# Row-wise infinity norm: most loads moved from SyncE to GpSimd, one packet per DMA engine and load

## The chip, the cores and the metric

The kernel runs on one core of a Trainium2 chip. The metric is the device time of one execution in microseconds, lower being better. The kernel before took 627.58 us, the median of three runs (627.51 to 627.71).

The engines are called PE (TensorE), DVE (VectorE), ACT (ScalarE), POOL (GpSimd) and SP (SyncE). SP computes nothing here; it issues DMA transfers. Sixteen DMA engines move the data from HBM into SBUF, the on-chip memory of 128 partitions.

## The reference

```python
def setup_inputs():
    return {
        "x": np.random.randn(8192, 8192).astype(np.float32),
    }

def reference(x: np.ndarray) -> np.ndarray:
    return np.linalg.norm(x, ord=np.inf, axis=1)
```

With `axis=1` this is a vector norm: for each of the 8192 rows, the largest absolute value of its 8192 columns. The input is 8192 x 8192 x 4 bytes = 268.44 MB, the output 32 KB. Every byte is read once and takes part in one comparison.

## The kernel before

Each partition holds 64 rows of x: 46 from a first group and 18 from a second one (`GROUPS`). "Row 0 to 63" below means the row within a partition; one row for all 128 partitions is 4 MB. The rows pass through a ring of 3 x 16384 floats per partition. `WHOLE` and `LAST` give the widths of the loads in columns, and behind each width the parts that ScalarE and GpSimd take over from VectorE near the end.

```python
GROUPS = [46, 18]
WHOLE = (
    [(8192, ())] * 2 + [(16384, ())] * 29 + [(16384, (3712, 3680)), (8192, (2016, 1984))]
)
LAST = [
    (3920, (1680,)), (1984, (848,)), (1040, (432,)), (576, (240,)), (320, ()), (352, ())
]
RING = 3 * 16384
```

One load is one DMA of 128 partitions, and for each partition one run of `w` floats that lie together in HBM (64 KB for 16384 columns). The last 352 columns go into a tile of their own, beside the partial results.

```python
    def load(pos, w):
        row = pos // n_cols
        a = pos - first[row] * n_cols
        if pos + w == R * n_cols:
            buf = last[:, :w]
        else:
            at = loads[-1][0] + loads[-1][1] if loads else 0
            if at + w > RING:
                at = 0
            buf = ring[:, at : at + w]
        inst = nc.sync.dma_start(out=buf, in_=x_of[first[row]][:, a : a + w]).ins
        ...   # cut: dependencies between loads that the reduces order anyway
        return buf
```

VectorE reduces each piece with one instruction (`absmax`, a tensor_reduce with max over absolute values). It is line 68 in the profile, the load is line 108.

```python
    pos = 0
    for u, (w, g) in enumerate(WHOLE):
        buf = load(pos, w)
        ...   # cut: row and number of rows
        if whole:
            red = absmax(
                res[:, row : row + whole],
                buf[:, : whole * n_cols].rearrange("p (c m) -> p c m", m=n_cols),
            )
        if g:
            ...   # cut: the last two whole loads are shared with ScalarE and GpSimd

    n = LAST[-1][0]
    for h, (w, g) in enumerate(LAST[:-1]):
        buf = load(pos, w)
        pos += w
        shared(last[:, n : n + 1 + len(g)], buf, g)
        n += 1 + len(g)

    load(pos, LAST[-1][0])
    absmax(res[:, R - 1 :], last)
    final = nc.sync.dma_start(out=out_of[first[-1]][:, GROUPS[-1] - 1 :], in_=res[:, R - 1 :])

    for f, o in out_of.items():
        k = min(o.shape[1], R - 1 - f)
        early = keep(nc.scalar.dma_start(out=o[:, :k], in_=res[:, f : f + k]))
        ...   # cut: a scheduling order against `final`
```

A load of 16384 columns can only be issued when the reduce of the load three before it has freed its part of the ring. The helper `keep` holds an instruction in program order; the loads of SP are not held by it, so the scheduler may move one that waits for nothing.

Of the kernel before, what the change touches and what calls it, by code (L numbers as in the profile page):

```python
# [1 line left out]

# [4 lines left out]

P = 128
FP32 = mybir.dt.float32
INT32 = mybir.dt.int32  # L10
MAX = mybir.AluOpType.max
X = mybir.AxisListType.X
ABS = mybir.ActivationFunctionType.Abs
# [11 lines that stand above are left out]
    (3920, (1680,)), (1984, (848,)), (1040, (432,)), (576, (240,)), (320, ()), (352, ())  # L25
]
RING = 3 * 16384


@with_exitstack  # L30
def kernel(
    ctx: ExitStack,
    tc: tile.TileContext,
    x: bass.AP,
    out: bass.AP,
):
    nc = tc.nc
    n_rows, n_cols = x.shape
    R = n_rows // P
    assert R == sum(GROUPS) and n_cols == 8192  # L40
    keep = tc.keep_in_program_order


    first = []
    x_of, out_of = {}, {}
    for k in GROUPS:
        f = len(first)
        x_of[f] = x[f * P : (f + k) * P].rearrange("(p r) m -> p (r m)", r=k)
        out_of[f] = out[f * P : (f + k) * P].rearrange("(p r) -> p r", r=k)
        first += [f] * k  # L50

    single = ctx.enter_context(tc.tile_pool(name="single", bufs=1))

    ring = single.tile([P, RING], FP32)
    res = single.tile([P, R], FP32)

    n_parts = sum(1 + len(g) for w, g in LAST[:-1])
    last = single.tile([P, LAST[-1][0] + n_parts], FP32)

    def not_before(inst, other, why):  # L60
        tc.add_manual_dep(
            inst.ins, other.ins.name,
            mybir.DependencyInfo(mybir.DependencyClass.Sync, mybir.DependencyReason.DATA),
            reason=why,
        )

    def absmax(dst, src):
        return keep(nc.vector.tensor_reduce(  # L68
            out=dst, in_=src, axis=X, op=MAX, apply_absolute_value=True,
        ))  # L70

    def max_pool(dst, src):

        pool = nc.gpsimd
        keep(pool.add_instruction(  # L75
            mybir.InstTensorReduce(
                name=nc.get_next_instruction_name(),
                ins=[pool.lower_ap(src.bitcast(INT32))],
                outs=[pool.lower_ap(dst.bitcast(INT32))],
                op=MAX,  # L80
                axis=X,
            )
        ))

    def shared(part, buf, g):

        a = buf.shape[1] - sum(g)
        red = absmax(part[:, :1], buf[:, :a])
        for i, c in enumerate(g):
            keep(nc.scalar.activation(buf[:, a : a + c], buf[:, a : a + c], ABS))  # L90
            max_pool(part[:, 1 + i : 2 + i], buf[:, a : a + c])
            a += c
        return red

    loads = []
# [9 lines that stand above are left out]
            if at + w > RING:  # L105
                at = 0
            buf = ring[:, at : at + w]
        inst = nc.sync.dma_start(out=buf, in_=x_of[first[row]][:, a : a + w]).ins  # L108
        if pos + w < R * n_cols:
            if (len(loads) + 4) % 10 < 5:  # L110


                for b, v, earlier in loads:
                    if b < at + w and at < b + v:
                        tc.declare_no_dep(
                            inst, earlier, reason="ordered by the reduces in between",
                        )
            loads.append((at, w, inst))
# [6 lines that stand above are left out]
        row, k = pos // n_cols, w // n_cols  # L125
        pos += w
        whole = k - 1 if g else k
# [6 lines that stand above are left out]
            part = single.tile([P, 1 + len(g)], FP32, name=f"part{u}")  # L134
            shared(part, buf[:, whole * n_cols :], g)
            max_pool(res[:, row + whole : row + k], part)
        if u == 1:

            not_before(
                keep(nc.scalar.activation(res[:, :1], res[:, :1], ABS)),  # L140
                red, "not before the second row is in",
# [9 lines that stand above are left out]

    load(pos, LAST[-1][0])
    absmax(res[:, R - 1 :], last)
    final = nc.sync.dma_start(out=out_of[first[-1]][:, GROUPS[-1] - 1 :], in_=res[:, R - 1 :])


    for f, o in out_of.items():
        k = min(o.shape[1], R - 1 - f)
        early = keep(nc.scalar.dma_start(out=o[:, :k], in_=res[:, f : f + k]))
        tc.add_manual_dep(  # L160
            early.ins, final.ins.name,
            mybir.DependencyInfo(
                mybir.DependencyClass.NoSync, mybir.DependencyReason.SCHED_ONLY
            ),
            reason="takes the later semaphore",
        )


# [1 line left out]
_INS = ['x']  # L170
_OUTS = [((8192,), 'float32')]


# [23 lines left out]
```

## Time and profile before

| What | Value |
|---|---|
| Time, median of three runs | 627.58 us |
| Span of the profiled execution | 625.7 us |
| Bytes read from HBM | 268.44 MB |
| Mean rate over the span | 429 GB/s |
| VectorE busy | 536.7 us |
| First whole-row reduce starts | 12.85 us |
| Last reduce starts, lasts | 622.86 us, 0.53 us |

The profile page has the busy time of each engine, the span cut into 40 slices with a digit of busy tenths each, the DMA queues with their packets, and the chain of work that ended last, followed back from the final instruction. Below that stand groups of instructions: how often, the mean duration of one, and how long the engine sat idle before them and for whom. "Issue to landing" of a DMA runs from the instruction that starts it to the last of its completion signals. Times in the views count from the start of the span.

### The profile page before, as it was taken

How to read it: one execution, taken by the hardware profiler on the slowest of the kernel's cores; microseconds unless marked ns; L12 is line 12 of the kernel's file. 1: busy time of each engine (PE TensorE's matmuls, PEld its weight loads, DVE VectorE, ACT ScalarE, POOL GpSimd, SP SyncE). 2: the span in 40 equal slices, each digit the busy share in tenths (PEclk: the TensorE clock that was granted, in tenths of full speed). 3: DMA queues.
4: the chain of work that ended last, by engine and by line, in shares of the span. 5: the costliest groups of instructions: out<-in, count | busy, mean ns of one | idle time of the engine just before them, and what ended most of it. 6: DMA issues, size and time to landing. Idle time of an engine off the chain costs nothing.

```text
span 625.7 us, 175 instructions
## 1 busy us (share of the span) xinstructions
DVE 536.7 (86%) x40; ACT 15.1 (2%) x10; POOL 14.1 (2%) x14
## 2 busy tenths in 40 slices
DVE  1938988889888899888898888988889888899888
ACT  0000000000000000000000000000000000000044
POOL 0000000000000000000000000000000000000026
DMA  8999999999999999999999999999999999999997
GB/s 369 436 469 402 469 402 469 402 469 402 469 402 457 415 415 457 402 469 402 469 402 469 402 469 402 469 402 453 419 415 457 402 469 402 469 402 469 402 436 304
DMA packets 6048, 268.47 MB, mean 429 GB/s; under 512 B 1056, under 2 KB 1312, under 8 KB 1696
## 3 DMA queue, kind: packets, MB, share of 16 engines
q1 hardware_dynamic: 5760, 268.44, 99.3%
q10 hardware_dynamic: 288, 0.03, 0.0%
HBM read 268.44 MB, written 0.03 MB: 429 GB/s over the span
## 4 chain that ended last, share of the span: by engine, by line
DMA 71%; DVE 28%; SPq 0%; issue 0%; DVEq 0%
DMA ring<-in_x_dram 71%; DVE res L68 28%; DVE last L68 1%; SPq L108 0%; DVEq L68 0%
## 5 line engine op out<-in xcount | busy, mean ns | idle before, releaser
L68 DVE TENSOR_REDUCE res<-ring 128x2 f32<-128x16384 f32 (+1 forms) x32 | 525.4, 16420 | 86.4 <-DMA ring<-in_x_dram 86.4
L90 ACT ACTIVATE ring<-ring 128x3712 f32<-128x3712 f32 (+7 forms) x8 | 13.6, 1719 | 577.2 <-DMA ring<-in_x_dram 573.9
L75 POOL TENSOR_REDUCE part<-ring 128x1 int32<-128x3712 int32 (+3 forms) x4 | 10.1, 2562 | 607.6 <-ACT ring L90 607.6
L68 DVE TENSOR_REDUCE part<-ring 128x1 f32<-128x800 f32 (+1 forms) x2 | 5.5, 2748 | 0.1
L68 DVE TENSOR_REDUCE last<-ring 128x1 f32<-128x2240 f32 (+4 forms) x5 | 5.3, 1115 | 0.1
L75 POOL TENSOR_REDUCE last<-ring 128x1 int32<-128x1680 int32 (+3 forms) x4 | 3.4, 855 | 0.6 <-ACT ring L90 0.4
L140 ACT ACT_TABLE_LOAD x1 | 1.3, 1283 | 0.7 <-PEq L181 0.7
L140 ACT ACTIVATE res<-res 128x1 f32<-128x1 f32 x1 | 0.2, 203 | 29.3 <-DVE res L68 29.3
L68 DVE TENSOR_REDUCE res<-last 128x1 f32<-128x361 f32 x1 | 0.5, 529 | 0.1
L75 POOL TENSOR_REDUCE res<-part 128x1 int32<-128x3 int32 x2 | 0.4, 198 | 0.1
L181 POOL MEMSET const-float32-0.0<- 128x1 f32 x1 | 0.1, 99 | 0.2 <-issue 0.2
L181 POOL MEMSET const-bfloat16-1.0<- 128x1 bf16 x1 | 0.1, 102 | 0.0
L181 POOL MEMSET const-uint8-127<- 128x1 uint8 x1 | 0.1, 101 | 0.0
L181 POOL MEMSET const-float32-1.0<- 128x1 f32 x1 | 0.1, 99 | 0.0
## 6 DMA issues: line engine op xcount, KB each, us to landing
ring<-in_x_dram SPq DMA_DIRECT2D x3, 4096.0 KB, 21.4
ring<-in_x_dram SPq DMA_DIRECT2D x1, 1960.0 KB, 35.4
ring<-in_x_dram SPq DMA_DIRECT2D x1, 992.0 KB, 37.4
ring<-in_x_dram SPq DMA_DIRECT2D x1, 520.0 KB, 38.2
ring<-in_x_dram SPq DMA_DIRECT2D x30, 40.8
ring<-in_x_dram SPq DMA_DIRECT2D x1, 288.0 KB, 38.4
last<-in_x_dram SPq DMA_DIRECT2D x1, 176.0 KB, 38.3
ring<-in_x_dram SPq DMA_DIRECT2D x1, 160.0 KB, 38.3
```

The lines of the kernel that those rows point to most:

```text
L68: return keep(nc.vector.tensor_reduce(out=dst, in_=src, axis=X, op=MAX, apply_absolute_value=True,))
L75: keep(pool.add_instruction(mybir.InstTensorReduce(name=nc.get_next_instruction_name(), ins=[pool.lower_ap(src.bitcast(INT32))], outs=[poo ...
L90: keep(nc.scalar.activation(buf[:, a : a + c], buf[:, a : a + c], ABS))
L140: keep(nc.scalar.activation(res[:, :1], res[:, :1], ABS)),
L181: nc = _bacc.Bacc("TRN2", target_bir_lowering=False, num_devices=1)
```

## The change

Three things change.

The loads of rows 0 to 51 are issued by GpSimd in place of SP, with `single_packet=True`: the eight pieces (one for each partition) that a DMA engine moves for a load are marked as one packet in place of eight.

The very first load is cut: SP loads its first 512 columns (`BRIDGE`) while GpSimd prepares the other 7680. SP also keeps the loads of the last 12 rows.

The order in which the three output stores are written down is turned around, and the manual scheduling order between them is dropped.

It is for the gaps between packets: the DMA engines are to move longer stretches without a break, and SP's small load is to bridge the time until GpSimd's first data flows.

```diff
+SOFT = 52 * 8192
+BRIDGE = 512
...
-        inst = nc.sync.dma_start(out=buf, in_=x_of[first[row]][:, a : a + w]).ins
+        src = x_of[first[row]][:, a : a + w]
+        if pos == 0:
+
+            inst = nc.sync.dma_start(out=buf[:, :BRIDGE], in_=src[:, :BRIDGE]).ins
+            loads.append((at, BRIDGE, inst))
+            at, w, buf_, src = at + BRIDGE, w - BRIDGE, buf[:, BRIDGE:], src[:, BRIDGE:]
+        else:
+            buf_ = buf
+        if pos < SOFT:
+
+            inst = keep(nc.gpsimd.dma_start(out=buf_, in_=src, single_packet=True)).ins
+        else:
+            inst = nc.sync.dma_start(out=buf_, in_=src).ins
...
-    final = nc.sync.dma_start(out=out_of[first[-1]][:, GROUPS[-1] - 1 :], in_=res[:, R - 1 :])
-
...
-        early = keep(nc.scalar.dma_start(out=o[:, :k], in_=res[:, f : f + k]))
-        tc.add_manual_dep(
-            early.ins, final.ins.name,
-            mybir.DependencyInfo(
-                mybir.DependencyClass.NoSync, mybir.DependencyReason.SCHED_ONLY
-            ),
-            reason="takes the later semaphore",
-        )
+        keep(nc.scalar.dma_start(out=o[:, :k], in_=res[:, f : f + k]))
+    keep(nc.sync.dma_start(out=out_of[first[-1]][:, GROUPS[-1] - 1 :], in_=res[:, R - 1 :]))
```

In the built program of the changed kernel SP's instructions stand in this order: the 512 columns, the last 352 columns of the input (they go into a tile of their own and wait for nothing), five loads of 16384 columns, one of 8192, the tail of 3920, 1984, 1040, 576 and 320 columns, and the final store. Before, the 352 columns were the last load of all.

## The prediction

> **What bounds the kernel now.** I read the page from the top: busy time by engine, the 40 slices, the DMA queues, then the chain that ended last; after that the waits, the instruction groups by shape, and the packet records of the trace for the cost of one packet.
>
> ```profile
> DVE 536.7 (86%) x40; ACT 15.1 (2%) x10; POOL 14.1 (2%) x14
> ...
> DMA  8999999999999999999999999999999999999997
> ...
> DMA packets 6048, 268.47 MB, mean 429 GB/s; under 512 B 1056, under 2 KB 1312, under 8 KB 1696
> ...
> q1 hardware_dynamic: 5760, 268.44, 99.3%
> ```
>
> VectorE is the busiest compute engine, but the row of nines says that the 16 DMA engines never rest, from the first slice to the last but one. One queue carries everything: 268.44 MB, which is the whole of x. The queue's packet time covers 99.3% of the span, so what is left to gain by filling holes is under 1%.
>
> ```profile
> 59.16 0.02 issue
> 59.17 40.78 DMA ring<-in_x_dram
> 99.95 0.02 issue
> 99.97 17.23 DVE res L68
> 117.20 0.02 issue
> ...
> 582.02 35.44 DMA ring<-in_x_dram
> 617.45 0.02 issue
> 617.47 5.30 DVE last L68 x5
> 622.77 0.03 DVEq L68
> 622.81 0.05 issue
> 622.86 0.53 DVE res L68
> ```
>
> In the chain of work (start, duration, what) the same pattern comes back every 58.05 us: a load that takes 40.78 us from issue to landing, then a reduce of 17.23 us that frees its third of the ring. 58.05 us is three loads, so one load of 128 x 16384 floats (8.389 MB) takes 19.35 us. The load is issued with 40.78 - 19.35 = 21.4 us of other loads still ahead of it in the queue; an issue that is a few us late leaves no hole. The chain shows VectorE at 28% only because a reduce sits between two issues, not because it limits.
>
> ```profile
> DVE res L68 <- DMA ring<-in_x_dram: 86.4, 32, 12.8
> ...
> L68 DVE TENSOR_REDUCE res<-ring 128x2 f32<-128x16384 f32 x29 | 499.4, 17220 | 70.3 <-DMA ring<-in_x_dram 70.3
> L68 DVE TENSOR_REDUCE last<-ring 128x1 f32<-128x2240 f32 x1 | 2.5, 2485 | 0.1
> ```
>
> Here the waits and the groups by shape: a reduce of 17.22 us per 19.35 us load, so VectorE waits 2.13 us for each load. It sets the end only after the 3920-column load has landed (617.45): from there its five tail reduces run without a hole until the final one.
>
> Now the packets. In the trace's records a packet of 65,536 bytes takes 2418 ns, one of 2304 bytes 93 ns, one of 1280 bytes 55 ns, the 4-byte one that ends a load on each engine 9 ns. From 1280 to 65,536 bytes the slope is (2418 - 55)/64,256 = 0.03677 ns per byte, 27.2 GB/s per engine, 435 GB/s for 16. What is left is a constant of about 8.3 ns per packet (55 - 47.1). Eight packets and the ending one make 8 x 2418 + 9 = 19,353 ns, the 19.35 us of the chain. So the whole loss against the rate inside a packet is 9 x 8.3 = 75 ns a load, 0.4%.
>
> **What the Trainium skill says.** "DMA: Bandwidth & Descriptors", section "Where 436 GB/s comes from", puts the ceiling of a core's 16 DMA engines at 435 GB/s; the slope above agrees. Its section "Why small descriptors are slow (HBM only)" gives a fixed overhead of about 3 cycles per packet, which joining descriptors into one packet amortizes, beside a descriptor cost that joining does not remove. At that page's 850 MHz three cycles are 3.5 ns, less than half of the 8.3 ns that I find, so an estimate from this page is that not all of it goes away. Section "Queues, rings and completion order" says that an engine takes turns between queues at the ends of packets; no trace of the kernel before has two load queues, so it is untested here. "SBUF — State Buffer", section "Who interferes with whom", says that a tensor_reduce on this chip never takes the port that GpSimd needs to write descriptors; before, no load comes from GpSimd, so the trace says nothing of it.
>
> **The change part by part.**
> 1. Joined packets. Rows 0 to 51 are 27 loads on GpSimd (one of 7680, one of 8192, 25 of 16384 columns). Each has 8 packets per engine and would have one. If the whole 8.3 ns goes for 7 of 8: 27 x 7 x 8.3 = 1.57 us. If only the page's 3.5 ns goes: 27 x 7 x 3.5 = 0.66 us. If the cost belongs to the descriptor: 0. I take the middle of the first two, 1.1 us. It is wholly on the path, since the loads are.
> 2. Issue. 27 issues leave SP (0.33 us each) for GpSimd, whose generation is slower. With 21.4 us of loads ahead of each one, nothing of it shows, except at the start.
> 3. The start. Before, SP issues at 0.74 us and the first packet starts at 1.74 us. After, SP still does this, with 512 columns: 8 packets of 2048 bytes per engine, 8 x (75.3 + 8.3) + 9 = 0.68 us. The order of the instructions shows one thing that the diff does not say: the load of the last 352 columns has no wait and is now SP's second instruction, ahead of all others. It adds 8 x 60 + 9 = 0.49 us on the engines (60 ns is its packet in the records). Together they cover 1.17 us, to about 2.9 us. GpSimd issues at about 0.74 us as well; if its first data comes within 2.2 us of that, there is no hole. I expect none, or 0.2 us.
> 4. The 352 columns moved to the front. The end was set by VectorE from the landing of the 3920 columns on. Their landing now has 352 columns more ahead of it: 352 x 512 bytes at 434 GB/s = 0.42 us. The tail reduces after it are unchanged (5.30 + 0.09 + 0.53 us), and the data behind it ends earlier, which VectorE can't use. So this costs 0.42 us, unless the start had a hole that it fills. The cut of the first load adds 8 packets and an end, 0.08 us.
> 5. The junction. SP issues row 52 while GpSimd's last load is still queued. If engines take turns by packet, one 64 KB packet of SP (2.42 us) goes ahead of that load, which lands 2.42 us later; the next, short of that packet, lands 16.9 us after it. VectorE (17.22 us a reduce) is late by some 2.4 us once and regains it at 2.13 us a load with five loads left; the engines do not stop. Cost 0.
> 6. The last outputs: SP's final 0.5 KB store is unchanged in place; 0.
>
> Sum: -1.1 + 0.42 + 0.08 + 0.1 for the start = -0.5 us, 627.1. Not credited in it are the ending packets: if they join the load's packet as well, 27 x 8.3 ns = 0.22 us more goes. And a hole at the start of 0.4 us without the 352 columns would make them free. I lean a little to that side: 626.7 us.
>
> **The rivals.**
> A. The cost is per descriptor, or reading descriptors from memory costs as much as the joining saves. Then the load stays at 19.35 us, and the sum is +0.4 to +0.6: 628.1 us. For it: the skill's split of the two costs. Against: the 4-byte packet alone costs 9 ns, which looks like a price per packet.
> B. The first GpSimd packet (7680 columns in one piece, 8 x 30,720 bytes, 9 us on an engine) begins before SP's eight small packets are done on some engine. With turns by packet, each remaining small one then waits for a whole load; the 512 columns would land after several loads, VectorE would start tens of us late, the ring would fill, and the engines would stop for one or two reduces (8.7 to 17.4 us): 636 to 645 us. For it: packet starts of the first load are spread by 0.58 us over the engines in the kernel before. Against: SP's instruction is short and GpSimd has to write its descriptors first, and the width of 512 looks chosen for this.
> C. GpSimd starts late, beyond 2.9 us: each us is a hole of a us on the DMA path. A start at 4 us would make 628 us.
> D. The junction stops the ring: a large packet holds back SP's loads long enough for VectorE to starve twice. The slack of 21.4 us speaks against it; 1 to 3 us at most.
>
> **Range and chances.** The best case is parts 1 whole plus the ending packets, 1.8 us, and no other cost: 625.8; with a better start 625.4. A and a late start give 628 to 629. The range of 625.4 to 629.6 us leaves out B, which I give 5%. Over 2% faster would be below 615.0 us, while 268.44 MB at 435 GB/s alone are 617 us: 1%. Over 2% slower is 640.1 us and needs the bad form of B: 4%.
>
> **What would show it.** Step 1: the distance between VectorE's reduces in the GpSimd stretch (19.35 us now; 19.29 if the whole cost goes, 19.35 under A). Step 2: no holes in the DMA row. Step 3: the first 128 x 8192 reduce starts at 12.85 us now; 12.9 to 13.6 with both small loads ahead, 20 or more under B; the rise up to there gives a late start. Step 4: no hole in VectorE after the 3920 columns. Step 5: one wait of about 4.5 us near row 52, then shorter ones. I am wrong if the distance rises above 19.35 us or if VectorE is left waiting at the start.

## The result, and the profile after

The changed kernel takes 637.9 us (637.68 to 638.23, four runs) against 627.64 us for the kernel before, measured beside it (627.51 to 627.92, four runs). The ratio is 1.0163, with a 95% interval of 1.0146 to 1.0181. It is 10.3 us slower; the prediction said 626.7, with a range up to 629.6.

First the page of the kernel after: VectorE's and the DMA engines' busy tenths in 40 slices, the bytes moved per slice, and the two load queues (packets, MB, share of 16 engines' time).

```profile
DVE  0938988889888889888899888898888807999998
...
DMA  9999999999999999999999999999999999899992
GB/s 357 437 453 412 445 449 412 457 408 449 420 441 453 404 457 408 449 429 433 453 404 457 408 449 441 420 457 400 457 412 445 445 416 457 346 461 416 441 404 114
...
q0 software_dynamic: 3888, 217.84, 79.2%
q1 hardware_dynamic: 2016, 50.60, 18.6%
```

Two things differ from the rows of before. VectorE has a 0 near the end, and after it nines nearly up to the end: an engine that first had nothing to do and then could not catch up. The DMA engines' rate falls to 346 GB/s in one slice and to 114 in the last: the loads are done before VectorE is. GpSimd's queue counts 3888 packets, 27 loads x 16 engines x 9. Eight data packets and an end per engine and load are still in the records, as before. That they are joined into one packet is what the change asks for; no line of this page shows it.

The timeline of VectorE in the kernel after (start, duration, and in brackets the idle time before and who ended it):

```profile
15.52 8.69 DVE L72 TENSOR_REDUCE res<-ring 128x1 f32<-128x8192 f32 x1 [15.52 <-DMA ring<-in_x_dram]
25.22 8.69 DVE L72 TENSOR_REDUCE res<-ring 128x1 f32<-128x8192 f32 x1 [1.02 <-DMA ring<-in_x_dram]
44.58 17.22 DVE L72 TENSOR_REDUCE res<-ring 128x2 f32<-128x16384 f32 x1 [10.67 <-DMA ring<-in_x_dram]
...
470.36 17.22 DVE L72 TENSOR_REDUCE res<-ring 128x2 f32<-128x16384 f32 x1 [2.14 <-DMA ring<-in_x_dram]
489.72 17.22 DVE L72 TENSOR_REDUCE res<-ring 128x2 f32<-128x16384 f32 x1 [2.14 <-DMA ring<-in_x_dram]
528.44 94.32 DVE L72 TENSOR_REDUCE res<-ring 128x2 f32<-128x16384 f32 x6 [21.50 <-DMA ring<-in_x_dram]
622.67 5.40 DVE L72 TENSOR_REDUCE part<-ring 128x1 f32<-128x800 f32 x2
...
633.31 0.53 DVE L72 TENSOR_REDUCE res<-last 128x1 f32<-128x361 f32 x1
```

And the same places in the kernel before:

```profile
12.85 8.69 DVE L68 TENSOR_REDUCE res<-ring 128x1 f32<-128x8192 f32 x1 [12.85 <-DMA ring<-in_x_dram]
...
41.92 17.22 DVE L68 TENSOR_REDUCE res<-ring 128x2 f32<-128x16384 f32 x1 [10.67 <-DMA ring<-in_x_dram]
...
486.99 17.22 DVE L68 TENSOR_REDUCE res<-ring 128x2 f32<-128x16384 f32 x1 [2.13 <-DMA ring<-in_x_dram]
506.34 17.22 DVE L68 TENSOR_REDUCE res<-ring 128x2 f32<-128x16384 f32 x1 [2.13 <-DMA ring<-in_x_dram]
```

The reader can take the whole loss from these lines. The start: 15.52 against 12.85, 2.67 us late. GpSimd's stretch: from 44.58 to 489.72 are 445.14 us for 23 loads; from 41.92 to 486.99 before are 445.07 us for the same 23. Nothing was saved and nothing lost. The handover to SP: VectorE waits 21.50 us where 2.13 us was the rule, 19.4 us too long. From there the reduces run without a hole to the end, and of the lateness of 2.67 + 19.4 = 22.1 us that leaves 10.45 (the last reduce starts at 633.31, before at 622.86). VectorE has made up 11.65 us: five waits of 2.13 us are 10.65, and another 1.0 us lies in the shorter steps between reduces that follow without a hole. The 10.45 us are the 10.3 us of the times.

The packet records of the kernel after show how the 19.4 us came about (columns: start of a stretch of 4.84 us, 64 KB packets started by GpSimd's queue, by SP's queue, all engines):

```
484.2   32    0
489.0   16   16
493.9   16   16
...
518.1   16   16
522.9    1   31
```

GpSimd's last load and SP's first one share the engines one to one, packet by packet. VectorE needs GpSimd's load first, but on the slowest engine both end together, at 528 us.

### The profile page after: what moved, and what is told of

Read it like the earlier page. It is cut to its first block, busy times and chain, and to the rows that moved or that the text cites. A ratio compares the mean times of both kernels' runs of the same rounds, so it can differ in the third digit from the quotient of the medians.

```text
span 636.2 us, 184 instructions
## 1 busy us (share of the span) xinstructions
DVE 536.0 (84%) x40; ACT 15.0 (2%) x10; POOL 28.2 (4%) x41
## 3 DMA queue, kind: packets, MB, share of 16 engines
q0 software_dynamic: 3888, 217.84, 79.2%
## 4 chain that ended last, share of the span: by engine, by line
DMA 63%; DVE 33%; another core or an unknown queue 3%; issue 0%; POOL 0%; DVEq 0%; PEldq 0%
DMA ring<-in_x_dram 63%; DVE res L72 31%; DVE part L72 1%; DVE last L72 1%; POOL ring L122 0%; DVEq L72 0%; PEldq L200 0%
## 5 line engine op out<-in xcount | busy, mean ns | idle before, releaser
L122 POOL DMA_DIRECT2D ring<-in_x_dram x27 | 14.4, 533 | 454.2 <-DVE res L72 302.8
## 6 DMA issues: line engine op xcount, KB each, us to landing
ring<-in_x_dram POOLq DMA_DIRECT2D x25, 40.5
```

The costliest lines, as they stand in the source:

```text
L122: inst = keep(nc.gpsimd.dma_start(out=buf_, in_=src, single_packet=True)).ins
```

## The experiments

The theory after this reading had three parts: (1) the flag changes neither the pace nor the taking of turns; (2) at the start some DMA engines get no work in time; (3) at the handover the queues take turns piece by piece, and VectorE has too few loads left to regain the lateness. In every comparison the kernel before was timed beside the experiment.

**The flag alone.**

```diff
-            inst = keep(nc.gpsimd.dma_start(out=buf_, in_=src, single_packet=True)).ins
+            inst = keep(nc.gpsimd.dma_start(out=buf_, in_=src)).ins
```

> The changed kernel with single_packet dropped, all else as changed. Theory (the flag changes neither the pace nor the taking of turns; the cost of some 8 ns belongs to each 64 KB piece): 637.9 us, within 0.3 us of the changed kernel; 64 KB pieces at 2418 ns in both; VectorE waits 21.5 us once near row 52. Rival 1 (the flag saves part of it, hidden behind the other losses): 638.5 to 639.5 us. Rival 2 (the flag itself delays the start, because a DMA engine gets its first work only when a whole packet is written): under 636.5 us, with the first reduce starting 1 us or more before 15.52 us.

Measured: 638.22 us (637.98 to 638.44), ratio to before 1.0172 (1.0155 to 1.0189), so 0.3 us above the changed kernel, at the edge of what I expected; the runs of the two kernels overlap (637.68 to 638.23 with the flag). VectorE's timeline without the flag:

```profile
15.85 8.69 DVE L72 TENSOR_REDUCE res<-ring 128x1 f32<-128x8192 f32 x1 [15.85 <-DMA ring<-in_x_dram]
...
489.98 17.22 DVE L72 TENSOR_REDUCE res<-ring 128x2 f32<-128x16384 f32 x1 [2.13 <-DMA ring<-in_x_dram]
528.68 94.32 DVE L72 TENSOR_REDUCE res<-ring 128x2 f32<-128x16384 f32 x6 [21.48 <-DMA ring<-in_x_dram]
```

The 0.3 us stand already in the first line. They are too small to be put down to the flag: the first reduce of three experiments below, with the flag and the same first loads, starts anywhere from 15.31 to 15.77 us. The stretch from there to 489.98 is no longer than with the flag, and the wait of 21.48 us is the same; in the records both queues again start 16 pieces of 64 KB in each 4.84 us of sharing. With eight pieces per load the flag shows no effect, on the pace or on the turns. GpSimd's queue has 3888 packets in the records without the flag too, so their count does not show whether pieces were joined.

**A wait at the handover.** SP's first load waits for the landing of GpSimd's last; SP's loads are held in order, save the 352 columns.

```diff
+            if pos == SOFT:
+                not_before(made, lastsoft[0], "not beside the last load of GpSimd")
```

> SP's first load (rows 52 and 53) waits until GpSimd's last load has landed, so that the two never share the DMA engines; SP's loads kept in program order. Theory (the large loss is that the two queues take turns piece by piece, so that the load VectorE needs first lands 19.4 us late): although a wait is added, the time falls to 631.5 to 633 us, that is the time before plus 2.7 us of the start plus a hole of about 2 us; VectorE's long wait near row 52 falls from 21.5 to about 2 us and one of about 4 us follows. Rival (handing over from one queue to the other costs this in itself, or GpSimd's stretch leaves the ring behind): 636 us or more.

Measured: 633.36 us (633.2 to 633.83), ratio 1.0096 (1.0081 to 1.0111). A wait was added and the kernel became 4.5 us faster than the changed one. In VectorE's timeline:

```profile
509.32 17.22 DVE L72 TENSOR_REDUCE res<-ring 128x2 f32<-128x16384 f32 x1 [2.11 <-DMA ring<-in_x_dram]
531.10 17.22 DVE L72 TENSOR_REDUCE res<-ring 128x2 f32<-128x16384 f32 x1 [4.55 <-DMA ring<-in_x_dram]
550.46 17.22 DVE L72 TENSOR_REDUCE res<-ring 128x2 f32<-128x16384 f32 x1 [2.14 <-DMA ring<-in_x_dram]
```

The long wait is gone. In its place VectorE waits 4.55 - 2.11 = 2.4 us longer once. By the packet records most DMA engines have ended GpSimd's last load by 506.2 us, the slowest ends it at 508.8, and SP's first bytes move at 510.3, so all of them stand idle for 1.5 us. The time is 0.4 us above the range that I expected: the hole costs 2.4 and not 2.0, and in this run the start was 3.0 us late (509.32 against 506.34 before). Sharing was the cause of the lateness, not the handover as such.

**The handover far from the end.** `SOFT = 12 * 8192`: GpSimd issues rows 0 to 11 only.

> GpSimd issues rows 0 to 11 alone, SP the other 52. Theory (the handover makes VectorE 19.4 us late, and it regains 2.13 us with each load of 16384 columns, so that after ten loads nothing of it is left): 630.0 to 631.5 us, the time before plus 2.7 us of the start and at most one short hole in the DMA row; VectorE waits about 21 us once near row 12, then hardly at all for nine or ten loads, then 2.1 us again. Rival 1 (a handover costs the same wherever it stands): 637 to 638 us. Rival 2 (the loss is spread over the loads of GpSimd): 5 of 26 loads' share of 10 us, 629.5 us, with no long wait.

Measured: 631.28 us, but with a wide spread, 629.71 to 632.65 in four runs; ratio 1.0061 (1.0042 to 1.008). VectorE's timeline:

```profile
102.61 17.22 DVE L72 TENSOR_REDUCE res<-ring 128x2 f32<-128x16384 f32 x1 [2.31 <-DMA ring<-in_x_dram]
141.31 154.23 DVE L72 TENSOR_REDUCE res<-ring 128x2 f32<-128x16384 f32 x9 [21.48 <-DMA ring<-in_x_dram]
296.36 17.22 DVE L72 TENSOR_REDUCE res<-ring 128x2 f32<-128x16384 f32 x1 [0.82 <-DMA ring<-in_x_dram]
315.71 17.22 DVE L72 TENSOR_REDUCE res<-ring 128x2 f32<-128x16384 f32 x1 [2.13 <-DMA ring<-in_x_dram]
```

The same wait of 21.48 us stands here, and it costs nearly nothing: nine reduces without a hole make it up. At 315.71 the kernel is 2.9 us behind the kernel before (312.83), of which 2.5 us are the start. So the price of a handover is the lateness less what VectorE can regain before the end. Why the times spread by 2.9 us was not followed; only one of the four runs has a trace.

**Everything on SP.** `SOFT = 0`: the cut of the first load and the order of the stores stay, GpSimd issues no load, and the 352 columns come last.

> The first load cut at 512 columns and the stores in the changed order, but every load on SP; here the 352 columns come last again. Theory (the cut costs eight more pieces and one more end on each engine, 0.08 us, and nothing else remains of the change): 627.6 to 627.8 us, first reduce at 12.9 us. Rival (the cut or the order of the stores carries part of the loss): 628.5 us or more.

Measured: 627.5 us (627.47 to 627.81), ratio 1.0002 (0.9993 to 1.0011). The cut and the stores cost nothing that can be measured.

**A wider bridge.** `BRIDGE = 2048` in the changed kernel, nothing else.

> The changed kernel with SP's first piece of 2048 columns in place of 512, nothing else. Theory (up to five DMA engines have no work between 3.65 and 5.2 us, because GpSimd's descriptors reach them late; the slowest sets the landing of every later load): the first reduce starts at 13.3 to 13.8 us instead of 15.52, and the time falls by as much, to 635.7 to 636.3 us, as the lateness is carried to the end. Rival (loads from GpSimd land later for another reason, a later completion signal or slower first packets): first reduce at 15 us or later, 637.5 us or more.

Measured: 635.79 us (635.65 to 635.88), ratio 1.0133 (1.0116 to 1.015). The windows of the first microseconds (window, length, busy time of VectorE, ScalarE and GpSimd, clock, DMA share, GB/s), in the changed kernel and with the wider bridge:

```profile
3.70:5.70 2.00, 0.00 (x0) 0.00 (x0) 0.00 (x0) 1.00 0.71 276
```

```profile
3.70:5.70 2.00, 0.00 (x0) 0.00 (x0) 0.00 (x0) 1.00 1.25 516
```

In the changed kernel the engines are busy for 71% of the two microseconds after SP's small loads have ended at 3.65 us; by the packet records 11 of 16 work at 3.70 us and all 16 only at 5.2 us. SP with 2048 columns has work for all of them until then. (A share above 1 comes from packets that overlap in the records.) VectorE's timeline with the wider bridge:

```profile
13.28 8.69 DVE L72 TENSOR_REDUCE res<-ring 128x1 f32<-128x8192 f32 x1 [13.28 <-DMA ring<-in_x_dram]
...
526.12 94.32 DVE L72 TENSOR_REDUCE res<-ring 128x2 f32<-128x16384 f32 x6 [21.48 <-DMA ring<-in_x_dram]
```

The first reduce starts at 13.28 instead of 15.52, 2.24 us earlier, and the time falls by 2.1 us. The long wait at the handover, 21.48 us, is unchanged.

**Small pieces at the handover.** SP's load of rows 52 and 53 is cut into four of 4096 columns, 16 KB pieces; the other loads are as in the changed kernel, save that SP's are held in program order. The 352 columns are not held and stay in front.

```diff
+            n = 4096 if pos == SOFT else w
+            for c in range(0, w, n):
+                made = nc.sync.dma_start(out=buf_[:, c : c + n], in_=src[:, c : c + n])
+                if pos + w < R * n_cols:
+                    keep(made)
...   (cut: each part is entered in the list of loads)
```

> The load of rows 52 and 53, SP's first after GpSimd's stretch, is cut into four loads of 4096 columns, 16 KB pieces. Theory (the queues take turns piece by piece, whatever the size): each of the eight 64 KB pieces of GpSimd's last load then waits for one of 0.61 us instead of 2.42; VectorE's long wait falls from 21.5 us to about 7.0 us (2.1 + 8 x 0.61), this is regained in the loads that follow, and the time is 630.0 to 631.0 us (the time before, 2.7 us of the start, 0.2 us for 24 more pieces). Rival 1 (each queue gets half of the bandwidth): the wait stays at 21 us, 637.5 us or more. Rival 2 (turns by whole loads): the wait is 2.1 + 4.8 us at most but in one lump before the first piece.

Measured: 630.97 us (630.8 to 631.13), ratio 1.0056 (1.0041 to 1.0071).

```profile
489.65 17.22 DVE L72 TENSOR_REDUCE res<-ring 128x2 f32<-128x16384 f32 x1 [2.13 <-DMA ring<-in_x_dram]
513.91 51.47 DVE L72 TENSOR_REDUCE res<-ring 128x2 f32<-128x16384 f32 x3 [7.04 <-DMA ring<-in_x_dram]
567.28 17.22 DVE L72 TENSOR_REDUCE res<-ring 128x2 f32<-128x16384 f32 x1 [1.91 <-DMA ring<-in_x_dram]
```

The wait is 7.04 us where turns by piece gave 7.0 (2.1 + 8 x 0.61). Half of the bandwidth for each queue would have left it at 21. Three reduces later the rhythm of 2.1 us is back, and the time is 6.9 us below that of the changed kernel.

**Both repairs, and the order of the 352 columns.** First the bridge of 2048 and the four pieces together:

> Both repairs together: 2048 columns on SP first, and the load of rows 52 and 53 in four. Theory (start and handover are the whole loss, and the GpSimd stretch itself brings nothing): 628.1 to 628.9 us, that is the time before plus 0.4 us for the 352 columns moved to the front, 0.3 us for extra pieces and 0 to 0.4 us of the start that is left. Rival (the GpSimd stretch does save the 1.1 us of the prediction, hidden until now): 627.0 us or less.

Measured: 628.76 us (628.67 to 628.98), ratio 1.0021 (1.0013 to 1.0029). Then the same with SP's loads kept in program order:

```diff
-                if pos + w < R * n_cols:
+                if True:
                     keep(made)
```

> As the kernel before it, with SP's loads kept in program order, so that the 352 columns come last again. Theory (the end is set by VectorE from the landing of the 3920 columns on, and these now have 352 columns less ahead of them): 0.3 to 0.5 us less than with the 352 columns in front, 627.7 to 628.4 us. Rival (the 352 columns in front fill time in which DMA engines have nothing else to do): no difference, or up to 0.4 us more.

Measured: 628.27 us (628.1 to 628.37), ratio 1.0012 (1.0006 to 1.0019). The 352 columns in front cost 0.49 us, once the start has no hole that they could fill. With all repairs the kernel is still 0.8 us behind the kernel before: 0.06 us at the start (first reduce at 12.91), some 0.2 us for the 24 further pieces and three ends, and about 0.4 us after the last reduce. For these the trace offers a reading that no run tested: at the end SP checks semaphores one after another, and five such checks, 0.06 us apart, follow the one at which its last store has landed, where before none does at that place; this is 0.3 of the 0.4 us. GpSimd's stretch has brought nothing to set against them.

**The disputed cost by itself.** GpSimd's loads of two rows are issued as two loads of one row in pieces of 8 KB, so that an engine has 64 pieces where it had 8. If the flag saves a cost of each piece, it must show here.

```diff
+            if w == 16384:
+                to = buf_.rearrange("p (c r m) -> p r c m", r=2, m=2048)
+                come = src.rearrange("p (r c m) -> p r c m", r=2, m=2048)
+                inst = keep(nc.gpsimd.dma_start(out=to[:, 0], in_=come[:, 0], single_packet=True)).ins
...
+                buf_, src = to[:, 1], come[:, 1]
```

> The changed kernel, but each of GpSimd's 25 loads of two rows is issued as two loads of one row in pieces of 8 KB (32 pieces for each engine and load, the two rows interleaved in the ring, and VectorE reads them back in that order), with single_packet. 65 to 66 pieces on each engine for 8.389 MB in place of 8 or 9. Theory (the flag changes nothing, the constant belongs to the piece): 64 pieces of 8192 bytes at 301 + 8.3 ns and two ends are 19.8 us, so reduces in GpSimd's stretch are 19.8 us apart, and the time is 648 to 650 us, the same as without the flag. Rival (the flag joins the pieces of a load into one packet and saves the constant; with eight pieces this was too small to see): 19.3 us apart, at least 10 us less than without the flag.

> The same as the run with 8 KB pieces, without single_packet. Both theories: reduces 19.8 us apart in GpSimd's stretch, 648 to 650 us; 8 KB pieces at about 310 ns in the records. The theory expects no difference to the run with the flag; the rival 10 us or more.

Measured: 671.04 us with the flag (670.67 to 671.4), 671.09 without (670.79 to 671.67). VectorE's timeline with the flag:

```profile
482.73 17.22 DVE L155 TENSOR_REDUCE res<-ring 128x2 f32<-128x16384 f32 x1 [2.65 <-DMA ring<-in_x_dram]
502.61 17.22 DVE L155 TENSOR_REDUCE res<-ring 128x2 f32<-128x16384 f32 x1 [2.66 <-DMA ring<-in_x_dram]
561.14 94.32 DVE L155 TENSOR_REDUCE res<-ring 128x2 f32<-128x16384 f32 x6 [41.31 <-DMA ring<-in_x_dram]
```

and without it:

```profile
482.84 17.22 DVE L155 TENSOR_REDUCE res<-ring 128x2 f32<-128x16384 f32 x1 [2.67 <-DMA ring<-in_x_dram]
502.72 17.22 DVE L155 TENSOR_REDUCE res<-ring 128x2 f32<-128x16384 f32 x1 [2.66 <-DMA ring<-in_x_dram]
561.28 17.22 DVE L155 TENSOR_REDUCE res<-ring 128x2 f32<-128x16384 f32 x1 [41.33 <-DMA ring<-in_x_dram]
```

The reduces are 19.88 us apart in both: 0.52 us more than with 64 KB pieces, for 57 pieces and ends more, 9.2 ns each. The flag saves none of it. The time missed my 648 to 650 us by 21, because I had not carried the theory through to the handover: there GpSimd's 8 KB pieces take turns with SP's 64 KB pieces and so get a ninth of the bytes. The packet records with the flag have 112 starts of each queue between 526 and 547 us. SP's next two loads go through before GpSimd's last one gets on, and the wait is 41.3 us instead of 21.5. This 19.8 us and 25 x 0.52 = 13 us are the 33 us above the changed kernel. It is the small pieces at the handover turned round.

## Why the prediction was wrong

*What bounds the kernel* held: 433 and 434 GB/s in the middle (100 to 480 us), where neither kernel gains.

*Step 1, joined packets, -1.1 us*, failed: it is 0. The wrong term is "each has 8 packets per engine and would have one", with a price on the seven that go. `single_packet` takes nothing off the pace, with 8 pieces a load (19.35 us) or with 64 (19.88 us). Rival A forecast the right distance, 19.35 us; its reason, a cost that joining leaves in place, is not shown. The runs allow as well that the pieces were never joined: the turns at the handover change at every piece, with the flag as without it. I took "one packet per engine and load" from the change's intention and priced it; the evidence that I named against rival A, that the 4-byte piece alone costs 9 ns, can't tell a price per packet from one per piece. The price has a slip too: 55 - 47.1 is 7.9 ns, and it is the packet of 2304 bytes that leaves 8.3; with 7.9 the 1.57 us would be 1.49. The estimate of 0.66 us that I worked out from the Trainium skill ("DMA: Bandwidth & Descriptors", section "Why small descriptors are slow (HBM only)") isn't borne out by these runs either. That section also says that joining is only worth it for descriptors of at most 256 bytes, which I passed over: the pieces here have 64 KB, and 8 KB where the experiment cut them.

*Step 2, the issue is hidden*, held: an issue takes GpSimd 0.53 us and SP 0.33, but GpSimd's loads take 40.5 us from issue to landing, SP's took 40.8, and the reduces in between keep their distance.

*Step 3, the start, 0.1 us beside the small loads*, was mis-sized. I let GpSimd issue at 0.74 us and its data come at one moment, before 2.9 us. It issued at 1.27 us; the first of its data came at 3.14 us, but some engines had none until about 5.2 us, and a load has landed when its slowest engine is done (of GpSimd's last load 12 engines are done by 523.7 us, the slowest at 527.96, and VectorE starts at 528.44). The first reduce was 2.67 us late, of which I had expected 0.57 for the small loads. The wider bridge moved this reduce forward by 2.24 us. Rival C had the mechanism, if not the spread over engines; rival B did not occur.

*Step 4, the 352 columns, +0.42 us*, held, as a term: 0.49 us between the two kernels that differ in nothing else, and from the first reduce on (13.47 and 12.91), as every load stands behind these columns. In the changed kernel it is not to be seen: there VectorE runs without a hole from the handover to the end, and at the start the 352 columns sat where some engines had nothing else (a reading; no run has the narrow bridge with the 352 columns last).

*Step 5, the junction, 0 us*, is the step that failed most: 7.6 us of the 10.3 (the 2.7 of the start taken off); the small pieces at the handover returned 6.9. In place of one wait of 4.5 us VectorE had one of 21.5. Nor did the DMA engines keep going: SP could issue its third load of two rows only at 545.68 us, when VectorE had freed the ring, and at 546 us 4 of the 16 moved data. The step rested on step 1. If GpSimd's last load were one packet for each engine, one SP piece of 2.42 us could slip in ahead of it, and the lateness would be 2.4 us. Since turns go by piece, eight slip in: 8 x 2.42 = 19.4 us. I had the rate at which VectorE regains, 2.13 us a load with five loads left, and so could have seen that 10.7 us, and no more than 11.65 as measured, is all there is to regain. Rival D had the place right, but I bounded it at 3 us by the slack of 21.4 us between an issue and its turn. That slack protects against late issues; it is the very stretch in which the other queue's load cuts in.

*Step 6, the stores*, held (627.5 us with all loads on SP).

## What to carry to other kernels

With the DMA engines full, a load from a second queue did not stand behind the loads of the first here; it took turns with them, piece by piece (16 and 16 starts of 64 KB in 4.84 us), and delayed just the load that was needed next, by 19.4 us. Hand over with small pieces on the new queue, or early enough that the consumer's slack can make it up, and work out both the lateness and the slack that is left. Before pricing a flag, try it alone on a load where its effect would be large: 64 pieces with and without it said more than any count of records.

## What the runs showed of the hardware that was not expected

- A wait added before SP's first load made the changed kernel 4.5 us faster, though it left all DMA engines idle for 1.5 us and made VectorE wait 2.4 us longer there.
- Turns between two load queues go by piece and not by bytes: 64 KB waiting on 64 KB made VectorE wait 21.5 us, 64 KB waiting on 16 KB 7.0 us, 8 KB waiting on 64 KB 41.3 us.
- `single_packet` on GpSimd's loads changed neither the pace (445.14 and 445.07 us for 23 loads) nor the turns, and left 671.04 against 671.09 us with 64 pieces. Whether it joined anything, these runs do not show.
- GpSimd's four first issues are done 2.24 us after they start at 1.27 us, but the DMA engines begin on its data between 3.14 and about 5.2 us.
